# Attention: exponentials and combination a step later, in front of the next scores, on four one-bank PSUM tiles

## The chip, the cores and the metric

The kernel runs on one core of a Trainium2 chip. The metric is device time in microseconds (us) of one execution; lower is better. The engines are PE (TensorE matmul, with PEld its weight loads), DVE (VectorE), ACT (ScalarE), POOL (GpSimd) and SP (SyncE, which here issues DMAs).

## The reference

Two layers of a diffusion transformer over 512 image tokens and 256 context tokens of width 1024. Layer 0 mixes tokens by differential attention, layer 1 by a gated scan (HGRN2); each layer has a SwiGLU FFN before and behind the mixer. The change concerns layer 0's attention, with 8 heads, each of two maps of key width 64 and values of width 128:

```python
def attend(q, k, v):
    s = jnp.einsum('bqhmd,bkhmd->bhmqk', q, k).astype(jnp.float32) * scale
    p = jax.nn.softmax(s, axis=-1)
    a = (p[:, :, 0] - lam * p[:, :, 1]).astype(v.dtype)
    return jnp.einsum('bhqk,bkhe->bqhe', a, v)

def finish(o):
    o = rmsnorm(o, subln) * (1 - lam_init)
    return o.reshape(bsz, o.shape[1], DA_WIDTH) @ w_o

k_all = jnp.concatenate([k_l, k_c], axis=1)      # image tokens, then context
y_l = finish(sweep_query_blocks(lambda qb: attend(qb, k_all, v_all), q_l))
y_c = finish(attend(q_c, k_c, v_c)) if need_ctx else None
```

Queries are taken in blocks of 128. The four image blocks see all 768 keys ("wide" below), the two context blocks only the 256 context keys ("narrow"). Before attention q, k and v are projected, and q and k of the image tokens are rotated (RoPE).

## The kernel before

Matmuls are of fp32 precision put together from halves: every operand is split into a high part (an fp32r cast, on ScalarE, `split`) and a low part (the difference, on VectorE, `low`), and each product is three passes, high by high, high by low, low by high. Weights come by DMA in the order of a list of jobs (`J`); a job's splitting is done when it is asked for (`J.need`) or by `work()` ahead of need, as far as `J.limit` lets it.

Attention goes by pairs of heads, p = 0 to 3. The main line of the program is the projection of q, k and v of pair p (lines L593 and L1190), each 512 columns into a one-bank PSUM tile `tp`. Rotations of q and k (`rot`, L1137 to L1141) are VectorE's, the copy of the context part (`cx`, L1147) ScalarE's. Under it runs the attention of the pair before, as a generator `attn(p, vh)`, which a `Ticker` T moves on by one step for each T.every us of main-line matmuls (by the program's own count). `T.later(x, f)` calls f when x us more have been counted. The last pair's attention runs in this way under the output stage, `o_groups`, whose matmuls (L681) multiply the finished heads `on` (in `hT` and `hl` parts) by the output weight `wo`; in its part for y the products stand in `tp` tiles, which ScalarE or VectorE adds up in `y` (L694, L698).

`attn` has 12 items, two heads hh by six query blocks t, and takes three steps for each; a period is one item. In the kernel before:

- Step 1: the scores of item idx, two maps, each in a two-bank PSUM tile `mm` (L989, L995); the row maxima `nm` on VectorE (L999); the exponentials `pt` on ScalarE (L1004), which read the scores from PSUM and need the maxima. Then the value product of an earlier block if one is due (`av`, L1048, with its copy `of`, L1053), and the low parts that were put off (`settle`).
- Step 2: the transposes of item idx - 1 (L1031), six of 128x128 in two `tp` tiles, their high casts `aT` on ScalarE (L1033) and low parts on VectorE (L1037). These read `tp` from PSUM, so a tile is free when its low part is done.
- Step 3: the combination of item idx: reciprocal `rc` (L1013), factor `c1` (L1015), and pt[0] += c1 * pt[1] (L1016), all on VectorE; then a value weight's splitting, and `work()`.

So transposes already stand a period behind their scores. `finish` (L1061 to L1079) is the norm of a head: squares, their sums by TensorE, a power on GpSimd, and a broadcast product.

PSUM has eight banks of 2 KB a partition. All through the program they are two `mm` tiles of two banks, three `tp` tiles of one, and one tile `gv` of one bank, of which the value product uses one half and the norm the other. A tile is handed out again when its last reader is done. Each engine works in program order; the order is set by the generator's steps and by where T stands on the main line.

## Time and profile before

| what | value |
|---|---|
| time, median of 3 runs | 3121.38 us (3120.86 to 3123.49) |
| profiled execution | 3116.74 us |
| its span, first to last instruction | 3114.9 us |
| mean granted TensorE clock | 0.989 |
| PE busy | 3003.0 us, 96% of the span |
| PEld busy | 2703.4 us, 87% |
| DVE busy | 1718.1 us, 55% |
| ACT busy | 951.6 us, 31% |
| attention with scores in it | about 664 to 1060 us of the span |

The profile is of one execution. "Busy" is the time in which an engine works on something; the rest is idle, and a row says in brackets how long an engine idled before it and which instruction (engine, tile, line) ended the idle time. L12 is line 12 of the kernel; a name such as `tp<-hT,hl` says which tile is written from which. The granted clock is a share of TensorE's full speed; the levels seen here are 0.50 and 1.00, other values are means over a stretch that holds both.

### The profile page before, as it was taken

Reading aid. Unit: us, or ns where it says so; the run is one execution under the profiler, and the core shown is the slowest. Engines: PE = TensorE matmul, PEld = TensorE weight load, DVE = VectorE, ACT = ScalarE, POOL = GpSimd, SP = SyncE. Lnnn points to the kernel's source line nnn. Section 1 sums busy time; section 2 is a strip of 40 time slices with the busy share of each in tenths; the row PEclk is TensorE's granted clock in tenths of the full one; section 3 lists DMA queues with packets and bytes.
Section 4 is the critical chain, followed back from the end, with each engine's and each line's share of the span. In section 5 each row is a group of like instructions: output and inputs, shape, how many; then the busy total and the mean of one; then the engine's idle time right before and its main releaser. Section 6 shows DMA issues by size and latency. Waiting matters only on the chain.

```text
span 3114.9 us, 41080 instructions
## 1 busy us (share of the span) xinstructions
PE 3003.0 (96%) x17122; PEld 2703.4 (87%) x17122; DVE 1718.1 (55%) x2433; ACT 951.6 (31%) x1575; POOL 115.3 (4%) x187
## 2 busy tenths in 40 slices
PE   7999999999988999999999999999999999899998
PEld 5999999887876789999998999999889998678887
DVE  4555555656665774444448554444566475744344
ACT  4111111534444441111115111111544343442222
POOL 0000000100000100000001000000100000100000
PEclk9999999999999999999999999999999999999999
DMA  5333333245434323233222333333211110423231
GB/s 226 109 117 114 122 114 119 105 134 131 121 81 120 134 99 103 97 102 102 88 82 80 114 122 111 110 116 114 88 58 52 57 55 31 149 95 102 82 115 61
DMA packets 109546, 321.77 MB, mean 103 GB/s; under 512 B 11728, under 2 KB 12208, under 8 KB 109360
## 3 DMA queue, kind: packets, MB, share of 16 engines
q1 hardware_dynamic: 104432, 301.26, 30.1%
q0 software_dynamic: 3200, 11.59, 1.0%
q10 hardware_dynamic: 1728, 6.29, 0.5%
q8 instruction: 135, 2.21, 0.3%
q14 instruction: 51, 0.42, 0.0%
HBM read 292.83 MB, written 26.26 MB: 102 GB/s over the span
## 4 chain that ended last, share of the span: by engine, by line
PE 85%; DVE 5%; ACT 5%; issue 3%; DMA 1%; POOL 1%; SPq 0%; ACTq 0%; DVEq 0%; POOLq 0%
PE mm L602 34%; PE mm L681 21%; PE mm L593 9%; PE tp L593 5%; PE tp L602 3%; PE tp L1190 2%; PE tp L1423 2%; PE gv L1048 1%; PE tp L681 1%; PE mm L1333 1%; ACT pt L1004 1%; ACT tmp L564 1%; ACT tmp L414 1%; DVE nm L999 1%; PE mm L989 1%
## 5 line engine op out<-in xcount | busy, mean ns | idle before, releaser
L602 PE MATMUL mm<-hT,hl 128*128 128x384 f32 x6048 | 1067.3, 337 | 0.8 <-ACT tmp L773 0.8
L602 PEld LDWEIGHTS mm<-hT,hl 128*128 128x128 f32 x6048 | 1049.4, 188 | 9.7 <-issue 6.0
L681 PE MATMUL mm<-wo,a 128*128 128x512 f32 x2886 | 664.9, 390 | 0.5 <-DVE wo L194 0.5
L681 PEld LDWEIGHTS mm<-wo,a 128*128 128x128 f32 x2886 | 539.7, 188 | 115.6 <-DVE y L696 2.8
L698 DVE TENSOR_TENSOR y<-y,mm 128x1024 f32<-128x1024 f32 x163 | 199.1, 1221 | 496.8 <-PE mm L681 496.7
L194 DVE TENSOR_TENSOR hl<-raw,hl 128x1024 fp32r<-128x1024 f32 x250 | 302.5, 1221 | 138.2 <-ACT hl L203 137.8
L593 PE MATMUL mm<-hT,hl 128*128 128x512 f32 (+1 forms) x1680 | 335.2, 355 | 7.3 <-DVE hT L569 3.2
L593 PEld LDWEIGHTS mm<-hT,hl 128*128 128x128 f32 x1680 | 274.9, 190 | 60.1 <-DVE hT L569 6.8
L311 DVE SCALAR_TENSOR_TENSOR acc<-mw,cs,acc 128x512 f32<-128x512 f32 x392 | 271.7, 747 | 2.3 <-DMA mw<-in_w_mod_dram 0.7
L203 ACT CAST a<-tmp 128x768 fp32r<-128x768 f32 (+1 forms) x88 | 68.8, 781 | 660.1 <-DVE tmp L790 660.1
L203 ACT CAST hl<-raw 128x1024 fp32r<-128x1024 f32 x250 | 258.5, 1046 | 24.3 <-DMA raw<-in_w_in_dram 19.6
L593 PE MATMUL tp<-hT,hl 128*128 128x512 f32 (+1 forms) x1056 | 237.0, 371 | 15.5 <-DVE aT L1037 9.5
L203 ACT CAST wo<-raw 128x1024 fp32r<-128x1024 f32 x94 | 98.2, 1045 | 463.1 <-PE mm L681 457.7
L593 PEld LDWEIGHTS tp<-hT,hl 128*128 128x128 f32 x1056 | 173.5, 192 | 47.8 <-DVE aT L1037 11.4
L773 ACT ACTIVATE tmp<-mm 128x768 f32<-128x768 f32 (+1 forms) x88 | 66.8, 759 | 402.8 <-PE mm L602 339.8
L790 DVE TENSOR_TENSOR tmp<-tmp,mm 128x768 f32<-128x768 f32 (+1 forms) x88 | 78.0, 886 | 197.3 <-PE mm L602 141.6
L602 PE MATMUL tp<-hT,hl 128*128 128x384 f32 x768 | 147.1, 342 | 6.7 <-ACT F L1438 6.7
L602 PEld LDWEIGHTS tp<-hT,hl 128*128 128x128 f32 x768 | 131.3, 188 | 8.7 <-ACT F L1438 8.6
L1004 ACT ACTIVATE pt<-mm,nm 128x768 f32<-128x768 f32 (+1 forms) x96 | 72.4, 757 | 160.5 <-DVE nm L999 160.5
L194 DVE TENSOR_TENSOR a<-tmp,a 128x768 fp32r<-128x768 f32 (+1 forms) x88 | 78.5, 892 | 74.6 <-ACT a L203 74.6
L194 DVE TENSOR_TENSOR wo<-raw,wo 128x1024 fp32r<-128x1024 f32 x94 | 114.9, 1222 | 3.6 <-ACT wo L203 3.6
L681 PE MATMUL tp<-hl,hT 128*128 128x512 f32 x300 | 89.7, 432 | 13.6 <-DVE hl L194 6.3
(193 smaller groups left out, 2521.8 us busy)
## 6 DMA issues: line engine op xcount, KB each, us to landing
raw<-in_w_in_dram SPq DMA_DIRECT2D x176, 512.0 KB, 4.3
mw<-in_w_mod_dram SPq DMA_DIRECT2D x144, 512.0 KB, 4.3
raw<-in_w_out_dram SPq DMA_DIRECT2D x88, 512.0 KB, 3.2
raw<-in_hg_w_dram SPq DMA_DIRECT2D x32, 512.0 KB, 3.2
raw<-in_da_qk_dram SPq DMA_DIRECT2D x16, 512.0 KB, 3.5
gg<-gg_d POOLq DMA_DIRECT2D x12, 512.0 KB, 4.4
xp<-x_d SPq DMA_DIRECT2D x10, 512.0 KB, 8.1
raw<-in_da_v_dram SPq DMA_DIRECT2D x8, 512.0 KB, 3.3
```

The lines of the kernel that those rows point to most:

```text
L194: nc.vector.tensor_tensor(out=dst_lo, in0=src, in1=dst_hi.bitcast(F32), op=ALU.subtract)
L203: nc.scalar.copy(out=dst_hi, in_=src)
L311: nc.vector.scalar_tensor_tensor(out=acc[:, m], in0=raw[:, kk], scalar=cs[:, k, m:m + 1], in1=acc[:, m], op0=ALU.mult, op1=ALU.add)
L593: nc.tensor.matmul(out=ps_ap, lhsT=w[a], rhs=mv[b], start=(k == 0 and i == 0), stop=(k == nk - 1 and i == 2))
L602: nc.tensor.matmul(out=ps, lhsT=w[:, u, k], rhs=hT[:, k, v, a:b], start=(k == 0 and i == 0), stop=(k == KC - 1 and i == 2))
L681: nc.tensor.matmul(out=po if small else po[:, hh * 512:(hh + 1) * 512], lhsT=aT[ci][:, u, t * P:(t + 1) * P], rhs=wos[ci][:, v, hh * 512:( ...
L698: nc.vector.tensor_tensor(out=dst, in0=dst, in1=src, op=ALU.add)
L773: nc.scalar.activation(out=flat(sg, pgv), in_=pgv, func=AF.Silu)
L790: nc.vector.tensor_tensor(out=flat(sg, puv), in0=flat(sg, puv), in1=puv, op=ALU.mult)
L1004: nc.scalar.activation(out=pt[:, :n], in_=scs[m][:, :n], func=AF.Exp, bias=nms[m], accum_out=s0s[hh][:, t:t + 1] if m == 0 else s1)
L1190: nc.tensor.matmul(out=pv[:, tt], lhsT=hT[:, k, a, t * P:(t + 1) * P], rhs=wk[:, b], start=(k == 0 and i_ == 0), stop=(k == KC - 1 and i_ ...
L1423: nc.tensor.matmul(out=pv[:, tt], lhsT=hT[:, k, a, t * P:(t + 1) * P], rhs=wk[:, b], start=(k == 0 and i_ == 0), stop=(k == KC - 1 and i_ ...
```

## The change

Step 1 of the generator keeps scores and maxima, followed by `settle()` and then the value product. The exponentials move to the end of step 2, behind the transposes and casts of the item before, and the combination moves from step 3 to directly behind them. PSUM is dealt by stage: in attention there are two `mm` and four `tp` tiles and no `gv`; the value product and the norm take `tp` tiles. Before and behind that stage the deal is as it was. Beside this: the sums of the rotation are put off (0.3), its high and low parts go from 1.2 and 2.4 to 1.6 and 2.8; `wo(h)` is listed ahead of `on(h)`, for both mixers; J.limit is one higher in the last pair's projections; the output stage ticks every 35/56 instead of 34/56 us, and one step of the generator is called ahead of the first output matmul.

```diff
@@ -85,18 +85,27 @@
     def tmp(shape, dtype=F32):
         return cur["tmp"].tile(shape, dtype, tag="tmp", name="tmp")
 
-    mmp = ctx.enter_context(pool("ps_mm", 2, PSUM))
-    tpp = ctx.enter_context(pool("ps_tp", 3, PSUM))
-    gvp = ctx.enter_context(pool("ps_gv", 1, PSUM))
+    banks = {}
+
+    def deal(key, **bufs):
+
+        if "stack" in banks:
+            banks.pop("stack").close()
+        st = banks["stack"] = ExitStack()
+        for tag, n in bufs.items():
+            banks[tag] = st.enter_context(pool(f"ps_{tag}{key}", n, PSUM))
+
+    ctx.callback(lambda: banks.pop("stack").close())
+    deal(0, mm=2, tp=3, gv=1)
 
     def ps_mm(shape):
-        return mmp.tile(shape, F32, tag="mm", name="mm")
+        return banks["mm"].tile(shape, F32, tag="mm", name="mm")
 
     def ps_tp(shape):
-        return tpp.tile(shape, F32, tag="tp", name="tp")
+        return banks["tp"].tile(shape, F32, tag="tp", name="tp")
 
     def ps_gv(shape):
-        return gvp.tile(shape, F32, tag="gv", name="gv")
+        return banks["gv"].tile(shape, F32, tag="gv", name="gv")
 
     x_d = dram.tile([NT, P, D], F32, name="x_d")
     gg_d = [dram.tile([2, D], F32, name=f"gg_d{i}") for i in range(6)]
@@ -644,8 +653,8 @@
             J.add((tag + "wo", h), wsrc[h * P:(h + 1) * P, :], [P, D], conv_unit if h < TAIL else conv_wo, unit=h < TAIL)
 
         for h in range(TAIL):
+            wo(h)
             on(h)
-            wo(h)
         limits[tag + "o"] = len(J.jobs)
         for h in range(TAIL, HEADS):
             wo(h)
@@ -975,7 +984,7 @@
 
             s0s = {}
 
-            def scores_softmax(hh, t):
+            def scores(hh, t):
                 n = NTOK if t < LT else NCTX
                 st_ = stk[p, hh]
                 if t == 0:
@@ -998,6 +1007,10 @@
                     nm = sm.tile([P, 1], F32, tag="nm", name="nm")
                     nc.vector.tensor_reduce(out=nm, in_=scs[m][:, :n], axis=AX.X, op=ALU.max, negate=True)
                     nms.append(nm)
+                state[hh, t] = (scs, nms, s1, n)
+
+            def exps(hh, t):
+                scs, nms, s1, n = state[hh, t]
                 pts = []
                 for m in range(2):
                     pt = dp.tile([P, NTOK], F32, tag=f"p{m}", name="pt", bufs=2 - m)
@@ -1041,7 +1054,7 @@
             def av(hh, b):
 
                 aT = aTs.pop((hh, b))
-                ot = gv[:, 0]
+                ot = ps_tp([P, 256])
                 ks = list(range(NT)) if b < 2 else [LT, LT + 1]
                 for n_, kk in enumerate(ks):
                     for i_, (u, v) in enumerate(PASSES):
@@ -1062,13 +1075,14 @@
                 sq = dp.tile([P, NTOK], F32, tag="sq", name="sq", bufs=1)
                 nc.scalar.activation(out=sq, in_=of, func=AF.Square)
                 yield
-                ot = gv[:, 1]
+                ot = ps_tp([P, NT])
                 for j in range(NT):
                     nc.tensor.matmul(out=ot[:, j:j + 1], lhsT=sq[:, j * P:(j + 1) * P], rhs=ones, start=True, stop=True)
                 nc.vector.scalar_tensor_tensor(out=r, in0=ot[:, 0:NT], scalar=1.0 / P, in1=e, op0=ALU.mult, op1=ALU.add)
                 nc.gpsimd.tensor_tensor(out=r, in0=r, in1=halfc.to_broadcast([P, NT]), op=ALU.pow)
                 yield
                 for j0 in range(0, NT, 2):
+                    ot = ps_tp([P, 256])
                     for j in range(2):
                         nc.tensor.matmul(out=ot[:, j * P:(j + 1) * P], lhsT=r[:, j0 + j:j0 + j + 1].to_broadcast([P, P]),
                                          rhs=ident, start=True, stop=True)
@@ -1080,15 +1094,16 @@
 
             n = len(items)
 
+
             for idx in range(n + 2):
                 if idx < n:
-                    scores_softmax(*items[idx])
+                    scores(*items[idx])
+                settle()
                 if avs:
                     h2, b2 = avs.pop()
                     av(h2, b2)
                     if b2 == 2:
                         fin.append(finish(h2))
-                settle()
                 if idx == 0:
                     stack_q(p, 1)
                     stack_k(p, 1)
@@ -1098,9 +1113,10 @@
                     transp(h1, t1)
                     if t1 % 2 == 1:
                         avs.append((h1, t1 // 2))
+                if idx < n:
+                    exps(*items[idx])
+                    combine(*items[idx])
                 yield
-                if idx < n:
-                    combine(*items[idx])
                 if splits:
                     defer[0] = True
                     splits.pop(0)()
@@ -1121,11 +1137,11 @@
         avs = []
         fin = []
         splits = []
-        gv = ps_gv([P, 2, 256])
-
         T = Ticker()
         for p in range(NPAIR):
             T.every = 45.5 / 42
+            if p == NPAIR - 1:
+                J.limit += 1
             for wi, w in enumerate("qk"):
                 qs = 0.125 if w == "q" else 1.0
                 rot = {}
@@ -1136,15 +1152,16 @@
                     for j in range(2):
                         nc.vector.scalar_tensor_tensor(out=dst[:, j], in0=src, scalar=qs, in1=CSt[:, j ^ ab],
                                                        op0=ALU.mult, op1=ALU.mult)
-                    if ab:
-                        for j in range(2):
-                            nc.vector.tensor_tensor(out=rot[0][:, j], in0=rot[0][:, j], in1=dst[:, j],
-                                                    op=ALU.add if j else ALU.subtract)
 
                 def plain(ab, src, rot=rot, qs=qs):
                     if ab == 0:
                         rot["cx"] = pp.tile([P, 2, NCTX], F32, tag="cx", name="cx")
                     nc.scalar.activation(out=rot["cx"][:, ab], in_=src, func=AF.Copy, scale=qs)
+
+                def sums(rot=rot):
+                    for j in range(2):
+                        nc.vector.tensor_tensor(out=rot[0][:, j], in0=rot[0][:, j], in1=rot[1][:, j],
+                                                op=ALU.add if j else ALU.subtract)
 
                 def highs(rot=rot):
                     hl = rot["hl"] = pp.tile([P, 2, 2, NTOK], F32R, tag="qkhl", name="qkhl")
@@ -1168,6 +1185,8 @@
                         plain(ab, first[ab][:, NLAT:NTOK])
                         rotate(ab, first[ab][:, 0:NLAT])
                         continue
+                    if p == 0 and ab == 0:
+                        deal(1, mm=2, tp=4)
                     u = need_spread(("dqk", p, wi, ab), 2)
                     for (a0, a1) in ((0, NLAT), (NLAT, NTOK)):
                         pl = ps_tp([P, 512])
@@ -1176,8 +1195,9 @@
                             rotate(ab, pl)
                         else:
                             plain(ab, pl[:, 0:NCTX])
-                T.later(1.2, highs)
-                T.later(2.4, stored)
+                T.later(0.3, sums)
+                T.later(1.6, highs)
+                T.later(2.8, stored)
             vh = [dp.tile([P, NT, 2, P], F32R, tag="vh", name="vh", bufs=3) for _ in range(2)]
             wv = [J.need(("dv", p, 0)), need_spread(("dv", p, 1), 1)]
             for t2_ in range(NT // 2):
@@ -1209,11 +1229,13 @@
         cur["yo"] = y
         cur["oT"] = new_hT()
         J.limit = limits["do"]
-        T.every = 34.0 / 56
+        T.every = 35.0 / 56
+        T(T.every)
         outs = o_groups("d", [(0,), (1, 2), (3, 4)], "yo", NT, T)
         while T.gen is not None and next(outs, outs) is not outs:
             pass
         T.finish()
+        deal(2, mm=2, tp=3, gv=1)
 
     def mixer_tail(l, tag, si, nt, nxt, fp, xp, outs):
```

In TensorE's order nothing moves in the first three pairs, apart from the name of the tile of value products and norms. The three places below show the instructions as they stand in each engine's queue, with repeated ones counted.

First, ScalarE in the middle of pair 1, about 783 to 795 us of the trace before. L1004 (before) and L1017 (after) are exponentials, L1033 and L1046 casts of transposes, L1053 and L1066 copies of a value product, L203 and L212 casts of weights, L1147 and L1159 copies of a projection. Before:

```order
L1004 ACTIVATE pt,s_6176<-mm,nm 128x768
L1004 ACTIVATE pt,s_6373<-mm,nm 128x768
L1053 COPY of<-gv 128x256
L1033 CAST aT<-tp 128x3x128 x2
L203 CAST hl<-raw 128x1024
L1004 ACTIVATE pt,s_6176<-mm,nm 128x256
L1004 ACTIVATE pt,s_6460<-mm,nm 128x256
L1033 CAST aT<-tp 128x3x128 x2
L1147 ACTIVATE cx<-tp 128x256
```

After:

```order
L1066 COPY of<-tp 128x256
L1046 CAST aT<-tp 128x3x128 x2
L1017 ACTIVATE pt,s_6194<-mm,nm 128x768
L1017 ACTIVATE pt,s_6394<-mm,nm 128x768
L212 CAST hl<-raw 128x1024
L1046 CAST aT<-tp 128x3x128 x2
L1017 ACTIVATE pt,s_6194<-mm,nm 128x256
L1017 ACTIVATE pt,s_6481<-mm,nm 128x256
L1159 ACTIVATE cx<-tp 128x256
```

In each period the two exponentials have gone from ahead of the copy and the casts of the transposes to behind them.

Second, ScalarE where the output stage begins, at 955 us of the trace before; L694 and L703 empty output tiles into y, and the casts of `hT` and `hl` (L203, L212) split the finished heads and the output weight. Before:

```order
L1195 CAST vh<-tp 128x2x128 x2
L203 CAST hT<-raw 128x768
L203 CAST hl<-raw 128x1024
L1004 ACTIVATE pt,s_8158<-mm,nm 128x768
L1004 ACTIVATE pt,s_8159<-mm,nm 128x768
L694 COPY y<-tp 128x512 x2
L203 CAST hT<-raw 128x768
L203 CAST hl<-raw 128x1024
L1004 ACTIVATE pt,s_8158<-mm,nm 128x768
L1004 ACTIVATE pt,s_8221<-mm,nm 128x768
L694 COPY y<-tp 128x512
L1033 CAST aT<-tp 128x3x128 x2
```

After:

```order
L1215 CAST vh<-tp 128x2x128 x2
L1017 ACTIVATE pt,s_8198<-mm,nm 128x768
L1017 ACTIVATE pt,s_8199<-mm,nm 128x768
L212 CAST hT<-raw 128x768
L703 COPY y<-tp 128x512 x2
L212 CAST hl<-raw 128x1024
L212 CAST hT<-raw 128x768
L1046 CAST aT<-tp 128x3x128 x2
L1017 ACTIVATE pt,s_8198<-mm,nm 128x768
L1017 ACTIVATE pt,s_8255<-mm,nm 128x768
L703 COPY y<-tp 128x512 x3
```

The first exponentials now stand ahead of the cast of the first finished head, and the first output weight is no longer split here.

Third, TensorE at the same place: L1190 and L1210 are the last value projection, L681 and L690 output matmuls, L989 to L1004 scores. Before:

```order
L1190 MATMUL tp<-hl,hT 128x256 x27
L681 MATMUL tp<-hl,hT 128x512
L989 MATMUL mm<-stk 128x512
L989 MATMUL mm<-stk 128x256
L989 MATMUL mm<-stk 128x512
L989 MATMUL mm<-stk 128x256
L995 MATMUL mm<-stk 128x512 x2
L995 MATMUL mm<-stk 128x256 x2
L681 MATMUL tp<-hl,hT 128x512 x3
```

After:

```order
L1210 MATMUL tp<-hl,hT 128x256 x27
L998 MATMUL mm<-stk 128x512
L998 MATMUL mm<-stk 128x256
L998 MATMUL mm<-stk 128x512
L998 MATMUL mm<-stk 128x256
L1004 MATMUL mm<-stk 128x512 x2
L1004 MATMUL mm<-stk 128x256 x2
L690 MATMUL tp<-hl,hT 128x512 x2
```

The last pair's first scores have gone ahead of the first output matmul.

## Rows read from the trace of the kernel before

**Rows 1.** Windows of the two parts: us, busy by engine (instructions), PEclk, DMA share, GB/s

```profile
...
664.00:955.00 291.00, 266.07 (x1779) 231.21 (x1777) 186.46 (x347) 125.92 (x287) 9.72 (x10) 0.98 0.41 109
955.00:1060.00 105.00, 85.78 (x453) 67.25 (x453) 70.14 (x128) 48.38 (x102) 6.90 (x8) 0.92 0.28 81
...
```

**Rows 2.** TensorE's waits, 664 to 1060: us in total, times, longest us

```profile
...
PE tp L593 <- DVE aT L1037: 9.5, 6, 2.4
PE tp L1031 <- ACT y L694: 7.8, 3, 4.8
PE tp L593 <- ACT cx L1147: 4.1, 3, 1.8
PE tp L1031 <- ACT cx L1147: 3.6, 3, 1.7
PE tp L681 <- DVE aT L1037: 2.6, 4, 0.8
PE gv L1048 <- DVE r L1068: 2.4, 1, 2.4
PE tp L681 <- ACT hl L203: 2.4, 1, 2.4
PE tp L1031 <- DVE y L698: 2.0, 2, 1.8
PE mm L989 <- ACT pt L1004: 1.6, 2, 1.3
...
```

**Rows 3.** Windows at clock 0.50: first of four and sum, last of three and sum

```profile
...
686.12:689.53 3.41, 3.21 (x15) 3.21 (x16) 3.34 (x9) 0.00 (x0) 0.00 (x0) 0.50 0.48 159
...
sum 13.64, PE 13.32 PEld 12.42 DVE 9.80 ACT 3.08 POOL 1.33; mean PE 3.33 PEld 3.10 DVE 2.45 ACT 0.77 POOL 0.33
...
1013.80:1017.21 3.41, 3.41 (x12) 2.39 (x10) 2.94 (x7) 1.49 (x3) 0.00 (x0) 0.50 0.00 0
sum 17.06, PE 13.21 PEld 10.45 DVE 12.40 ACT 7.29 POOL 0.00; mean PE 4.40 PEld 3.48 DVE 4.13 ACT 2.43 POOL 0.00
```

**Rows 4.** Timeline, 780 to 800: start us, us, operation, [idle before it <- releaser]

```profile
...
782.72 1.82 DVE L999 TENSOR_REDUCE nm<-mm 128x1 f32<-128x768 f32 x2 [0.95 <-PE mm L995]
783.72 0.90 ACT L1004 ACTIVATE pt<-mm,nm 128x768 f32<-128x768 f32 x1 [4.31 <-DVE nm L999]
...
785.53 0.36 ACT L1053 COPY of<-gv 128x256 f32<-128x256 f32 x1
...
786.26 0.82 PE L1031 MATMUL tp<-ident,pt 128*128 128x128 f32 x6
786.78 0.86 ACT L1033 CAST aT<-tp 128x384 fp32r<-128x384 f32 x2 [0.89 <-PE tp L1031]
...
787.30 1.02 DVE L1037 TENSOR_TENSOR aT<-tp,aT 128x384 fp32r<-128x384 f32 x2 [2.75 <-ACT aT L1033]
...
788.68 1.02 DVE L1016 SCALAR_TENSOR_TENSOR pt<-pt,c 128x768 f32<-128x768 f32 x1
...
789.47 0.39 PE L989 MATMUL mm<-stk 128*128 128x256 f32 x2
...
794.97 2.63 PE L593 MATMUL tp<-hT,hl 128*128 128x512 f32 x6 [1.82 <-ACT cx L1147]
...
```

**Rows 5.** Groups by line on ScalarE, 664 to 1060: busy us, mean ns, idle before

```profile
...
L1004 ACT ACTIVATE pt<-mm,nm 128x768 f32<-128x768 f32 (+1 forms) x96 | 72.4, 757 | 160.5 <-DVE nm L999 160.5
...
```

**Rows 6.** Timeline of the output stage's start, 955 to 957

```profile
...
955.11 0.85 ACT L203 CAST hT<-raw 128x768 fp32r<-128x768 f32 x1
...
955.84 1.06 ACT L203 CAST hl<-raw 128x1024 fp32r<-128x1024 f32 x1
...
956.95 0.50 PE L681 MATMUL tp<-hl,hT 128*128 128x512 f32 x1 [2.41 <-ACT hl L203]
...
```

**Rows 7.** Timeline of TensorE in the output stage, at 1004 and 1013

```profile
...
1004.42 1.41 PE L681 MATMUL tp<-hl,hT 128*128 128x512 f32 x5
...
1013.09 0.55 PE L1031 MATMUL tp<-ident,pt 128*128 128x128 f32 x3 [1.78 <-DVE y L698]
...
```

## The prediction, made before the changed kernel had run

> **What bounds the kernel now.** I read the windows first, then the waits of TensorE inside them, then the granted clock, then one period in the timeline. Attention's scores run from about 664 to 1060 us. In its two parts TensorE is busy 266.07 of 291.00 us and 85.78 of 105.00 us [rows 1]: idle 24.9 and 19.2, together 44.1 us. VectorE is busy 186.46 and 70.14 us there and ScalarE less, so neither is the limit on the average; TensorE is, and what can be won is its idle time and its slow time. The waits say who ended the idle time [rows 2]: there are 17 rows of 43.9 us in all, the nine shown have 36.0 us. Six of the nine (9.5, 7.8, 4.1, 3.6, 2.6 and 2.0, together 29.6) are one thing: TensorE wants a one-bank PSUM tile ("tp") that ScalarE or VectorE has not yet emptied. Seven stretches stand at a granted clock of 0.50, that is 1.2 instead of 2.4 GHz; TensorE is busy 13.32 us in the four under the projections and 13.21 in the three of the output stage, 26.53 us in all, work that takes half of it at 2.4 GHz, so 13.3 us are lost [rows 3]. The last begins at 1013.80, 0.7 us after a wait of 1.78 us ended [rows 3, 7], the first at 686.12, beside one of the waits of 2.4; I take all of them for a consequence of the idle time. Ceiling of the stage: 44.1 + 13.3 = 57.4 us.
>
> Why the banks come late is to be seen in one period [rows 4]. The exponentials stand at 783.72 in ScalarE's queue as soon as the scores are written; they wait for the maxima (VectorE, 782.72, 1.82 us). Behind them stand the copy of the value product (785.53) and the casts of the transposes (786.78). In the next period the projection's own emptying (cx) stands behind them too, and TensorE idles 1.82 us for it (794.97). Summed up, ScalarE idles 160.5 us in front of exponentials [rows 5], and all that is queued behind them waits as well.
>
> **The change part by part.** *Exponentials behind the casts.* Row for row TensorE's order in the three pairs under the projections stays, so its work stays. ScalarE now empties the value product and the transposes first and does the exponentials after, when the maxima are long there; the emptying of projection (cx) and of output tiles (y) no longer stands behind a waiting instruction. Of the 29.6 us I leave 4: in the first period of the output stage two weight casts now stand ahead of the casts of the transposes, 1.06 + 0.85 us on ScalarE [rows 6], and their two low parts ahead on VectorE, for which I count 2.2 us of wait at the norm product; some 1.8 remain elsewhere. **Gain 25.6.**
>
> *What is late instead.* The scores' two tiles are freed only by the exponentials, which now start when the casts of the transposes end. From rows 4: last transpose ends 787.08, casts end 787.64, and two exponentials take 1.81 (783.72 to 785.53), so the second tile is free at 789.45 and, with 0.1 us for the release (it shows as 0.05 in rows 6: the cast ends at 956.90, the matmul starts at 956.95), at 789.55. The next scores begin at 789.47 and reach the second tile 0.2 to 0.4 later: hidden, with nothing to spare. Where fewer matmuls lie between, it shows: five output matmuls take 1.41 us [rows 7], against 2.4 needed. Counted by period: three of 0.25, one of 0.2, two of 0.85 and one of 0.4 in the output stage (3.1), some 0.3 in each of six periods under the projections (1.9). Together 5.0, in place of the 1.6 that the scores wait now. **Cost 3.4.** Bounds: zero, and at most 1.81 in each of the 32 wide periods, 58.
>
> *The combination directly behind them* (reciprocal, factor, 1.02 us of multiply-add) makes VectorE wait for the exponentials. Queued behind it are the rotations, the norm product and the next maxima. Per wide period: the low parts of the transposes end at 788.32, the exponentials at 789.45: 1.1 us of waiting, 32 times, and some 0.4 in 16 narrow ones, 42 us. VectorE's busy time is 256.6 of 396 us [rows 1], so it fits; the combination ends 789.45 + 1.4 = 790.9, as the next scores end, and the next transposes stand another 1.5 us behind that. I value this at zero. Bounds: if that cover goes, 42 us; gain: none, since no transposes wait for it now.
>
> *Four one-bank tiles, value product and norm in them too.* The product waited 2.4 us for the norm's reader because both lay in one tile [rows 2]; that goes. Cost of the added takers: I find the ones before each taker emptied at least a step earlier, so nothing. **Gain 2.4**, bounds 0 and 2.4.
>
> *Start of the output stage.* Now the first output matmul waits 2.41 us for casts that begin at 955.11 [rows 6]. After, the first scores come ahead of it, and on ScalarE the first exponentials ahead of the cast of the output's input. So after the scores TensorE waits for the first maximum (0.1 + 0.9), two exponentials (1.81), the cast (0.85) and the release: 3.8, and 0.4 more for its low part behind the combination. 4.2 instead of 2.4: **cost 1.8.** That the first weight is split beforehand hides nothing of it. In pair 0 a value weight's low part comes behind the combination: **cost 0.6.** Bounds for both: 0 and 6.
>
> *Sums, high and low parts of the rotation a little later, weight before input, a tick of 35 instead of 34:* VectorE and ScalarE work of the same length, used several us later; nothing.
>
> *The other waits* (7.9 us, the eight rows after the nine of the list) I leave as they are.
>
> *The clock.* If the stretches follow idle time, the four in the pairs go (half of 13.32 us, since hardly a wait is left there by the steps above), and of the three in the output stage one or two stay behind the 4.2 us: some 4 of 13.3 us remain. **Gain 9.3**, bounds 0 and 13.3.
>
> Sum: 25.6 − 3.4 + 2.4 − 1.8 − 0.6 + 9.3 = 31.5 us. The profiled execution took 3116.7 us; its sum is 3085.2. The median of the three timed runs lies 4.6 us above that execution, so the median to expect is 3089.9, say **3089 us**.
>
> **Rivals.** *The waits change their name (part of the gain).* The chain of scores, maxima, casts, exponentials, scores becomes the period. For it: the 0.0 to 0.1 us to spare in rows 4, and a collision or two per pair with a weight cast of 1.06 us [rows 6]. Against it: ScalarE is busy only 174 of 396 us. If the chain costs 0.5 us in each of the 32 wide periods (16 instead of 5) and half the clock loss stays (6.6 instead of 4), the gain is 31.5 − 11 − 2.6 = 17.9: 3103 us.
>
> *Everything goes.* All waits for tiles, the start, and the clock: 57.4 less the 7.9 of other waits: 49.5, 3072 us. For it: the order leaves slack in most places; against it the start of the output stage.
>
> *VectorE becomes the limit (the other side).* Place: the combination's wait in every wide period. If the maxima of the next scores come behind it so late that exponentials wait again, the exponentials lie bare between transposes and scores: 1.81 x 32 = 58 us, less the 29.6 + 2.4 that go in any case and with the clock as now: 26 us slower, 3147; the point from which it decides is about 1.1 us per wide period (32 x 1.1 = 35, what is won without the clock plus part of it). Against it: from rows 4 the first maximum could start at 790.9 + 0.9 = 791.8, and the exponentials behind it are not due before the casts of the next transposes (790.9 + 1.5 + 0.82 + 0.56 = 793.8): about 2 us of room, in which one queued operation of VectorE fits.
>
> *Nothing happens*, because TensorE's order in the pairs is the same and the waits are bound by VectorE's low parts (9.5 us of them) rather than by ScalarE: 3121. Against it: those low parts themselves idle for the casts behind the exponentials.
>
> *The room is larger than idle time.* On the rows, idle and slow time is all there is, since no matmul goes and none gets shorter. Weight loads are busy 231.21 + 67.25 = 298.5 of 396 us [rows 1], which would leave 97.5 us: 3117 − 97.5 + 4.6 = 3024. The Trainium skill (Perfetto Trace Analysis, "Identifying the Most-Contended Engine") says that TensorE's room is to be judged by the busy share of weight loads, not by that of matmuls. No run here shows that this room can be had; the change touches no matmul, and I give it 1 in 100.
>
> **How the numbers follow.** Forecast 3089 with a chance of 0.58; part of the gain, 3103, 0.22; everything, 3072, 0.12; VectorE as the limit 0.04; nothing 0.03; the larger room 0.01. The forecast's own range is 3081 to 3097. Between 3073 and 3107 lie the forecast, the part and most of the way to the full gain, some 8 in 10. About 0.2% (6 us) is what a measurement of this kernel can tell from no change: faster by more 0.91, within it 0.04, slower 0.05 (VectorE, and a bit of what I don't see).
>
> **What would show it.** Right: the waits of TensorE for "tp" tiles behind casts, cx and y fall from 29.6 us to some 4; the idle time of ScalarE before exponentials falls from 160.5 us to below 50; a new wait of the reciprocal for exponentials of some 40 us on VectorE; scores waiting for exponentials about 5 us; a wait of about 4 us at the first output matmul; the granted clock of 664 to 955 at 1.00. Wrong: scores waiting for exponentials 15 us and more, transposes waiting for the combination, a clock at 0.50 in the pairs without idle time ahead of it, or idle time that has moved behind 1060 us.

## The result

The changed kernel takes 3083.06 us (median of 4 runs, 3081.9 to 3085.34), the kernel before 3121.12 us (4 runs, 3118.22 to 3123.49): a ratio of 0.9886, 95% interval 0.9872 to 0.9899. (The two medians alone give 0.9878; in the later rounds the kernel before stands at 3117.97 to 3119.15 us, so the gain is rather 35 than 38 us.) The forecast was 3089 us, in a range of 3073 to 3107. The time came out within 6 us of the forecast; the largest of the reasons given for it held only in part.

The profiled execution took 3081.90 us, 34.8 less than that of before, with a span of 3080.1 us. Measured between the same matmuls of both traces, 0.5 us were won ahead of attention, some 25 in the three pairs under the projections, some 9 in the output stage, 0.3 behind it. The windows of the two parts, at the same places of the program as in [rows 1] (whose boundary of 955 is 954.5 by this count):

```profile
663.50:928.90 265.40, 259.65 (x1780) 227.21 (x1779) 186.65 (x348) 125.11 (x286) 10.11 (x10) 0.99 0.47 124
928.90:1025.50 96.60, 84.25 (x452) 64.00 (x452) 68.46 (x127) 47.42 (x102) 6.90 (x8) 0.96 0.25 78
```

The work is the same; TensorE's idle time went from 44.1 us in the two parts together to 5.8 and 12.4 us. Its waits, as in [rows 2]:

```profile
PE tp L1087 <- DVE aT L1050: 4.8, 5, 2.7
PE tp L690 <- ACT hT L212: 3.8, 1, 3.8
PE tp L1210 <- DVE aT L1050: 2.1, 2, 1.4
PE tp L1080 <- DVE y L707: 1.2, 1, 1.2
...
PE mm L998 <- ACT pt L1017: 0.8, 3, 0.3
```

All rows together make 17.8 us instead of 43.9. Waits for the projection's copies (cx) and for output tiles that ScalarE empties are gone, and so are waits of the q and k projections (L602) for low parts of transposes. New are the norm's broadcasts (L1087) that wait for low parts of transposes. Two stretches at a clock of 0.50 are left of seven [rows 3]:

```profile
674.40:677.82 3.42, 3.42 (x12) 2.26 (x11) 0.24 (x1) 0.00 (x0) 0.00 (x0) 0.50 0.45 153
933.82:940.64 6.82, 6.74 (x23) 5.72 (x25) 1.84 (x3) 0.61 (x2) 1.34 (x1) 0.50 0.26 85
sum 10.24, PE 10.16 PEld 7.98 DVE 2.08 ACT 0.61 POOL 1.34; mean PE 5.08 PEld 3.99 DVE 1.04 ACT 0.31 POOL 0.67
```

So 5.1 instead of 13.3 us are lost to the clock in this execution. The changed kernel was profiled a second time (run e5 below); there the waits make 17.1 us, but four stretches stand at 0.50:

```profile
sum 20.48, PE 19.62 PEld 14.35 DVE 7.33 ACT 3.70 POOL 2.69; mean PE 4.91 PEld 3.59 DVE 1.83 ACT 0.93 POOL 0.67
```

That is 9.8 us lost, and that execution took 3087.86 us: what the clock takes differs between executions of one kernel. Back to the first trace: the exponentials' idle time on ScalarE, against [rows 5], by line:

```profile
L1017 ACT ACTIVATE pt<-mm,nm 128x768 f32<-128x768 f32 (+1 forms) x96 | 72.6, 769 | 14.2 <-DVE nm L1008 14.2
```

And the period that answers to [rows 4], in the timeline of pair 1:

```profile
772.07 1.81 DVE L1008 TENSOR_REDUCE nm<-mm 128x1 f32<-128x768 f32 x2
...
774.09 0.37 ACT L1066 COPY of<-tp 128x256 f32<-128x256 f32 x1 [3.83 <-PE tp L1061]
775.28 0.82 PE L1044 MATMUL tp<-ident,pt 128*128 128x128 f32 x6
775.81 0.86 ACT L1046 CAST aT<-tp 128x384 fp32r<-128x384 f32 x2 [1.35 <-PE tp L1044]
...
776.55 0.92 ACT L1017 ACTIVATE pt<-mm,nm 128x768 f32<-128x768 f32 x1
...
777.44 0.92 ACT L1017 ACTIVATE pt<-mm,nm 128x768 f32<-128x768 f32 x1
...
778.48 0.16 DVE L1026 RECIPROCAL rc<-s 128x1 f32<-128x1 f32 x1 [1.14 <-ACT pt L1017]
778.49 0.40 PE L998 MATMUL mm<-stk 128*128 128x256 f32 x2
```

The copy of the value product and the casts come as soon as TensorE has written. The maxima end at 773.88, the exponentials begin 2.7 us later and wait for nothing; the second ends at 778.36, 0.1 us before the next scores begin, and the reciprocal waits 1.14 us for it.

### The profile page after: what moved, and what is told of

Its sections match the earlier page's. It is cut to its first block, busy times and chain, and to the rows that moved or that the text cites. A ratio compares the mean times of both kernels' runs of the same rounds, so it can differ in the third digit from the quotient of the medians.

```text
span 3080.1 us, 41105 instructions
## 1 busy us (share of the span) xinstructions
PE 2994.0 (97%) x17122; PEld 2694.4 (87%) x17122; DVE 1715.6 (56%) x2433; ACT 950.1 (31%) x1575; POOL 115.4 (4%) x187
## 4 chain that ended last, share of the span: by engine, by line
PE 86%; DVE 4%; ACT 4%; issue 3%; DMA 2%; POOL 1%; SPq 1%; ACTq 0%; DVEq 0%; POOLq 0%
PE mm L611 34%; PE mm L690 21%; PE mm L602 9%; PE tp L602 6%; PE tp L611 3%; PE tp L1445 2%; PE tp L1210 1%; PE tp L1061 1%; PE tp L690 1%; PE mm L1355 1%; ACT tmp L423 1%; ACT tmp L573 1%; PE mm L998 1%; DMA mw<-in_w_mod_dram 1%; PE mm L1004 1%
## 5 line engine op out<-in xcount | busy, mean ns | idle before, releaser
L690 PE MATMUL mm<-wo,a 128*128 128x512 f32 x2886 | 665.0, 390 | 0.5 <-DVE wo L203 0.5
L690 PEld LDWEIGHTS mm<-wo,a 128*128 128x128 f32 x2886 | 539.6, 188 | 115.7 <-DVE y L705 2.7
L203 DVE TENSOR_TENSOR hl<-raw,hl 128x1024 fp32r<-128x1024 f32 x250 | 302.3, 1220 | 141.4 <-ACT hl L212 141.2
L602 PE MATMUL mm<-hT,hl 128*128 128x512 f32 (+1 forms) x1680 | 334.2, 354 | 7.0 <-DVE hT L578 3.1
L602 PEld LDWEIGHTS mm<-hT,hl 128*128 128x128 f32 x1680 | 273.8, 189 | 59.8 <-DVE hT L578 6.9
L212 ACT CAST a<-tmp 128x768 fp32r<-128x768 f32 (+1 forms) x88 | 68.7, 781 | 659.9 <-DVE tmp L799 659.9
L212 ACT CAST hl<-raw 128x1024 fp32r<-128x1024 f32 x250 | 258.4, 1047 | 24.5 <-DMA raw<-in_w_in_dram 18.9
L212 ACT CAST wo<-raw 128x1024 fp32r<-128x1024 f32 x94 | 98.3, 1045 | 463.0 <-PE mm L690 457.7
L602 PE MATMUL tp<-hT,hl 128*128 128x512 f32 (+1 forms) x1056 | 232.4, 366 | 1.9 <-DVE hl L203 1.0
L602 PEld LDWEIGHTS tp<-hT,hl 128*128 128x128 f32 x1056 | 170.5, 188 | 31.9 <-issue 3.7
L203 DVE TENSOR_TENSOR a<-tmp,a 128x768 fp32r<-128x768 f32 (+1 forms) x88 | 78.5, 892 | 74.6 <-ACT a L212 74.6
L203 DVE TENSOR_TENSOR wo<-raw,wo 128x1024 fp32r<-128x1024 f32 x94 | 114.9, 1222 | 3.6 <-ACT wo L212 3.6
L690 PE MATMUL tp<-hl,hT 128*128 128x512 f32 x300 | 88.9, 426 | 9.6 <-ACT hT L212 4.0
L1008 DVE TENSOR_REDUCE nm<-mm 128x1 f32<-128x768 f32 (+1 forms) x96 | 70.1, 771 | 23.9 <-PE mm L1004 23.9
```

The costliest lines, as they stand in the source:

```text
L203: nc.vector.tensor_tensor(out=dst_lo, in0=src, in1=dst_hi.bitcast(F32), op=ALU.subtract)
L212: nc.scalar.copy(out=dst_hi, in_=src)
L602: nc.tensor.matmul(out=ps_ap, lhsT=w[a], rhs=mv[b], start=(k == 0 and i == 0), stop=(k == nk - 1 and i == 2))
L690: nc.tensor.matmul(out=po if small else po[:, hh * 512:(hh + 1) * 512], lhsT=aT[ci][:, u, t * P:(t + 1) * P], rhs=wos[ci][:, v, hh * 512:( ...
L1008: nc.vector.tensor_reduce(out=nm, in_=scs[m][:, :n], axis=AX.X, op=ALU.max, negate=True)
```

## The experiments

Each kernel was timed in five rounds beside the kernel before on its chip (4 to 11 runs each). What is compared is the ratio to that kernel; the changed kernel itself has 0.9886 and, in e5, 0.9892.

| run | what differs from the changed kernel | median us | ratio, 95% interval |
|---|---|---|---|
| e1_old_order | order of before | 3102.66 | 0.9948 (0.9934 to 0.9962) |
| e2_old_banks | PSUM deal of before | 3109.22 | 0.9968 (0.9957 to 0.9980) |
| e3_combine_third | combination in step 3 | 3081.37 | 0.9881 (0.9867 to 0.9894) |
| e4_late_exponentials | ScalarE copies ahead of exponentials | 3115.41 | 0.9992 (0.9983 to 1.0001) |
| e5_changed_again | nothing | 3084.39 | 0.9892 (0.9879 to 0.9906) |
| e6_rest_alone | order and deal of before | 3120.61 | 1.0007 (0.9998 to 1.0016) |
| e7_old_start | start of the output stage of before | 3084.85 | 0.9891 (0.9875 to 0.9906) |
| e8_input_first | first head split before first scores | 3081.04 | 0.9882 (0.9868 to 0.9895) |
| e9_old_rotation | times of the rotation's parts of before | 3085.69 | 0.9891 (0.9877 to 0.9906) |
| e10_old_jobs | jobs of before | 3084.70 | 0.9890 (0.9875 to 0.9905) |
| e11_input_first_norm_early | e8, norm's steps in step 1 | 3081.68 | 0.9880 (0.9865 to 0.9894) |
| e12_input_first_combine_third | e8 and e3 together | 3076.65 | 0.9866 (0.9850 to 0.9883) |

**e1: the old order, with four tiles.**

```diff
                     scores(*items[idx])
-                settle()
+                    exps(*items[idx])
...
+                settle()
...
+                yield
                 if idx < n:
-                    exps(*items[idx])
                     combine(*items[idx])
-                yield
```

> The changed kernel with ScalarE's and VectorE's old order alone: exponentials directly behind the maxima in step 1, combination in step 3, put-off low parts behind the value product. Four one-bank tiles and all else as changed. Theory A (the order on ScalarE is the cause): most of the gain goes, the exponentials idle more than 120 us for the maxima again, TensorE's waits for tp tiles come back to some 20 to 30 us, clock stretches at 0.50 come back in the pairs; 3108 to 3118 us. Rival B (the fourth one-bank tile is the cause, and takes up late casts): 3083 to 3092 us, waits for tp below 12 us.

TensorE's waits here:

```profile
PE tp L1044 <- ACT of L1066: 4.9, 4, 2.2
PE tp L690 <- ACT hT L212: 3.8, 1, 3.8
PE tp L1087 <- DVE aT L1050: 3.1, 5, 1.1
PE tp L690 <- ACT y L703: 2.5, 2, 1.4
PE tp L1087 <- ACT y L703: 2.5, 1, 2.5
```

Neither theory holds: 0.9948 lies between them, so the order is worth 17 to 19 us where the four tiles are in place. The exponentials idle 150.1 us for the maxima again, and ScalarE's emptying is late. But what VectorE ends, 19.5 us of the waits of before and 9.5 in the first row of [rows 2] alone, is 5.9 us here.

**e2: the old deal, with the new order.**

```diff
-                ot = ps_tp([P, 256])
+                ot = gv[:, 0]
...
-                ot = ps_tp([P, NT])
+                ot = gv[:, 1]
...
-                    if p == 0 and ab == 0:
-                        deal(1, mm=2, tp=4)
...
```

> The changed kernel with the old deal of PSUM alone: three one-bank tp tiles, and value product and norm in the two halves of one gv tile. Theory A: the product waits for the norm's reader again (2.4 and 0.9 us), projections have one tile less, while the 4.8 us that the norm's broadcasts wait for low parts in the changed trace go; 3081 to 3091 us. Rival B (the fourth tile is the cause): tp waits above 20 us, 3100 us or more.

```profile
PE tp L602 <- DVE aT L1050: 7.6, 5, 2.0
PE tp L690 <- DVE aT L1050: 5.3, 4, 2.5
PE gv L1061 <- DVE of L1089: 4.5, 5, 2.8
...
PE tp L1208 <- DVE aT L1050: 2.5, 4, 0.8
```

Again neither theory gives the time, and it lies nearer to the rival: 0.9968, so some 25 us of the gain need the new deal. The waits are VectorE's now: 15.4 us for low parts and 4.7 for the shared tile gv. One of them in the timeline of this run:

```profile
861.03 1.82 DVE L1008 TENSOR_REDUCE nm<-mm 128x1 f32<-128x768 f32 x2 [1.83 <-PE mm L1004]
861.73 0.81 PE L1044 MATMUL tp<-ident,pt 128*128 128x128 f32 x6
862.25 0.86 ACT L1046 CAST aT<-tp 128x384 fp32r<-128x384 f32 x2 [3.70 <-PE tp L1044]
862.77 1.22 DVE L203 TENSOR_TENSOR hl<-raw,hl 128x1024 fp32r<-128x1024 f32 x1
...
863.90 1.01 DVE L1050 TENSOR_TENSOR aT<-tp,aT 128x384 fp32r<-128x384 f32 x2
864.50 1.83 PE L602 MATMUL tp<-hT,hl 128*128 128x256 f32 x10 [1.96 <-DVE aT L1050]
```

The casts end at 863.1, early. The low parts, which free the two tiles of the transposes, stand on VectorE behind the maxima and a weight's low part until 863.90, and the projection wants its next tile 1.4 us before that. Here ScalarE is not what is late; with four tiles the projection has another one to take. The fourth tile and the parting of value product and norm were not timed apart.

The kernel before has nearly the same wait, with the old order, in its timeline at 866 to 870:

```profile
867.58 1.21 DVE L194 TENSOR_TENSOR hl<-raw,hl 128x1024 fp32r<-128x1024 f32 x1
868.64 0.85 ACT L1033 CAST aT<-tp 128x384 fp32r<-128x384 f32 x2
869.15 1.02 DVE L1037 TENSOR_TENSOR aT<-tp,aT 128x384 fp32r<-128x384 f32 x2 [0.36 <-ACT aT L1033]
869.76 1.12 PE L593 MATMUL tp<-hT,hl 128*128 128x256 f32 x6 [2.41 <-DVE aT L1037]
```

The casts stand behind the exponentials here, but VectorE is busy with a weight's low part until 0.36 us before it can take the transposes' own: of the 2.41 us that TensorE waits, earlier casts could have saved no more than that. In the four longest waits of the first row of [rows 2] (2.41, 2.41, 1.70 and 1.66 us) the low parts idle 0.35, 0.36, 0.36 and 1.44 us for the cast.

**e3: the combination in step 3**, exponentials where the change puts them.

```diff
                     exps(*items[idx])
+                yield
+                if idx < n:
                     combine(*items[idx])
-                yield
```

> The changed kernel with the combination in step 3 again, exponentials where the change puts them. The prediction valued the combination's place at zero. Theory A: 3080 to 3087 us; VectorE's wait of the reciprocal for exponentials falls from 26.5 us to under 10, TensorE's waits change by under 3 us in sum. Rival C (the combination's wait holds up the queue behind it): 2 to 8 us faster than the changed kernel. Rival D (the place counts the other way, transposes wait for the combination): 3090 us or more, with waits of transposes for pt.

0.9881 beside 0.9886 and 0.9892: the combination's place is worth nothing that can be measured, as theory A has it. Its number for VectorE missed: the reciprocal's wait fell only from 26.5 to 18.6 us, not below 10. Two transposes waited for the combination, 1.2 us in all.

**e4: exponentials made late** at six places.

```diff
                     pt = dp.tile([P, NTOK], F32, tag=f"p{m}", name="pt", bufs=2 - m)
+                    if m == 0 and p < NPAIR - 1 and (hh, t) in ((0, 2), (1, 1)):
+                        for _ in range(4):
+                            nc.scalar.copy(out=pt[:, :n], in_=scs[m][:, :n])
```

> The changed kernel with four copies of the scores (some 0.9 us each on ScalarE, overwritten by the exponentials behind them) ahead of the exponentials in two periods of each of the first three pairs, six places. In the changed trace the exponentials end 0.8 to -0.3 us before the next scores there. Theory A (nothing to spare, and slow clock follows idle time): next scores wait about 3.4 us at each place, 20 us in all, and stretches at 0.50 appear behind some of the six, 1.7 us each; 3103 to 3114 us. Rival E (slack is larger than it looks): under 10 us of new waits, below 3094 us. Rival F (the clock does not follow idle time): the waits come, but no stretch at 0.50 begins within 4 us behind them; 3100 to 3104 us.

The first place in TensorE's timeline, and three of the clock's windows:

```profile
688.95 0.61 PE L998 MATMUL mm<-stk 128*128 128x512 f32 x2 [2.37 <-ACT pt L1020]
689.83 1.01 PE L998 MATMUL mm<-stk 128*128 128x512 f32 x2 [0.27 <-ACT pt L1020]
```

```profile
689.72:696.55 6.83, 6.72 (x28) 5.85 (x29) 5.53 (x9) 0.43 (x2) 0.00 (x0) 0.50 0.01 2
727.26:730.67 3.41, 3.41 (x13) 2.54 (x14) 3.34 (x7) 2.44 (x4) 0.00 (x0) 0.50 0.01 2
...
819.42:826.25 6.83, 6.83 (x21) 4.78 (x22) 3.42 (x7) 1.88 (x4) 0.00 (x0) 0.50 0.18 39
```

The six waits are 2.37, 2.38, 2.31, 2.75, 1.59 and 2.74 us, 14.1 together: less than the 20 expected. The four copies took 3.32 us and not 3.6, and at the first place 2.37 + 0.27 us of that show, so 0.7 us were spare: the scores begin when the first of their two tiles is free, one exponential earlier than I had counted. At five of the six, all but that of 1.59, a stretch at 0.50 begins between 0.2 us ahead and 2.2 us behind the wait's end; TensorE is busy 27.03 us in these, 13.5 lost. So rivals E and F fall, and of theory A the mechanism holds, not the sizes: in these five the idle TensorE cost about as much again in clock. Five more stretches stand in this trace where nothing was copied, one at 846.73 and four in the output stage; TensorE is busy 23.1 us in them, against 10.2 in all of the changed kernel's. The time, 3115.41 us, lies 1 us above A's range.

**e5 and e6: the changed kernel again, and the rest alone.** e6 is the edits of e1 and e2 together.

> The changed kernel once more, on the chip of the three kernels below, as their measure: ratio to the kernel before 0.986 to 0.990.

> The changed kernel with both the old order on ScalarE and VectorE and the old deal of PSUM; what stays changed is the start of the output stage, the later sums and parts of the rotation, the order of the jobs and the tick of 35/56. From the runs before, order + rest gave some 9 us, tiles + rest some 16, all together some 36. Theory A2 (the rest is worth nothing, and order and fourth tile each need the other: a tile is late when either ScalarE's cast or VectorE's low part is late): within 4 us of the kernel before, tp waits ended by VectorE's low parts 10 to 16 us and by ScalarE's y and cx 12 to 18. Rival H (the parts simply add: order 20, tiles 27, so the rest costs 11): 8 to 14 us slower than before.

e5 repeats the changed kernel's time (0.9892). In e6 the rest is worth nothing (1.0007), so rival H falls. That each part needs the other, as theory A2 says, does not follow either: against e6 the order alone gives 0.0039 (12 us), the tiles alone 0.0059 (18 us), together 30 of some 36; what is left is within what the intervals leave open. The waits in attention say the same, by who ended them (us, over all rows of each run; "others" are casts and low parts of weights and heads, and GpSimd):

| kernel | by ScalarE's emptying | by VectorE's reading | others | PE busy at 0.50 |
|---|---|---|---|---|
| before | 18.6 | 19.5 | 5.8 | 26.5 |
| rest alone (e6) | 12.5 | 24.9 | 6.9 | 43.4 |
| order + rest (e2) | 2.9 | 25.7 | 7.2 | 23.7 |
| tiles + rest (e1) | 14.3 | 5.9 | 6.8 | 38.5 |
| all (changed) | 0.8 | 9.8 | 7.2 | 10.2 |

The order takes ScalarE's waits and leaves VectorE's; the tiles take VectorE's and leave ScalarE's. The columns show one execution each and do not give the times exactly: for the order alone, waits and half of the busy time at 0.50 fall by 18 us, where its timing gives 12.

**e7: the old start of the output stage.**

```diff
-        T.every = 35.0 / 56
-        T(T.every)
+        T.every = 34.0 / 56
```

> The changed kernel with the old start of the output stage: a tick of 34/56 us and no step of the generator ahead of the first output matmul. Theory (the prediction's term: the new start costs 1.8): the wait before the first output matmul is 2.4 instead of 3.8 us, 0 to 3 us faster than the changed kernel on the same chip. Rival: first scores behind the first matmul let later periods run closer together, 1 to 5 us slower.

The same time (0.9891 and 0.9892), so neither the theory's gain nor the rival's loss can be seen. The first wait fell to 1.5 us, but a wait of 2.4 us for low parts and one of 1.9 of scores for exponentials stand behind it:

```profile
PE mm L998 <- ACT pt L1017: 2.5, 3, 1.9
PE tp L690 <- DVE aT L1050: 2.4, 1, 2.4
...
PE tp L690 <- ACT hT L212: 1.5, 1, 1.5
```

**e8: the first head split ahead of the first scores.**

```diff
+        J.upto(J.pos["don", 0] + 1)
         T(T.every)
```

> The changed kernel, but the first finished head is split (cast of hT on ScalarE, low part on VectorE) ahead of the generator's step that stands before the first output matmul. TensorE's order stays. The wait of 3.8 us before that matmul goes to under 1, and the stretch at 0.50 that begins there (6.8 us, TensorE busy 6.74, so 3.4 lost) may go: 3 to 7 us faster than the changed kernel on the same chip. Rival: the first maxima and exponentials come about 1 us later and a wait behind them takes the place: within 1.5 us of it.

The wait went to 0.2 us, and the median is 3.4 us lower than e5's, but the intervals overlap: theory and rival stay undecided. Three stretches at 0.50 stand in the output stage all the same (13.7 us busy), the first at 932.43 with no wait above 0.3 us in the 9 us of TensorE's timeline ahead of it.

**e9 and e10: rotation and jobs as before.**

```diff
+                    if ab:
+                        for j in range(2):
...
-                T.later(0.3, sums)
-                T.later(1.6, highs)
-                T.later(2.8, stored)
+                T.later(1.2, highs)
+                T.later(2.4, stored)
```

```diff
+            on(h)
             wo(h)
-            on(h)
...
-            if p == NPAIR - 1:
-                J.limit += 1
```

> The changed kernel with the rotation's sums, high and low parts at their old times (sums with the rotation, 1.2, 2.4). The prediction valued the delays at zero. Theory: ratio to before 0.986 to 0.991, as the changed kernel (0.9886 and 0.9892). Rival: the two sums of 0.68 us again stand ahead of low parts of transposes on VectorE, and waits of tp tiles for VectorE grow by 4 us or more: 0.991 or above.

> The changed kernel with the finished head listed ahead of its output weight again and the jobs' limit not raised, so that the first output weight is split at the start of the output stage. The prediction valued this part at zero. Theory: the weight's cast (1.06 us on ScalarE) and low part come behind the cast of the head, the first wait grows by about 1 us, to 4.8: ratio 0.988 to 0.991. Rival: nothing beyond the noise, 0.987 to 0.989, first wait 3.8 still.

0.9891 and 0.9890: neither can be told from the changed kernel, and in e9 the waits of tiles for VectorE did not grow. In e10 the first wait is 4.7 us as expected, with 1.1 for the low part behind it.

**e11 and e12: two attempts to go on from e8.** e12 is the edits of e8 and e3; e11 is that of e8 and the following, where `work()`, in attention, does not split a job but moves a head's norm on by one step:

```diff
                         fin.append(finish(h2))
+                work()
...
                     defer[0] = False
-                work()
                 yield
```

> The kernel of the run with the first head's split ahead of the first scores, and the norm's steps moved from step 3 to step 1, behind the value product, so that its broadcasts no longer ask for a tile right behind the transposes. There these waited 4.3 us for low parts. Theory (the wait belongs to the place, two tiles being held by the transposes): it falls below 1 us, transposes wait at most 2 us more for the norm's product instead; 1 to 5 us faster than the changed kernel, ratio 0.985 to 0.988. Rival: the wait moves to the transposes in full, ratio 0.988 to 0.990.

> The first head's split ahead of the first scores, and the combination in step 3. Theory: the two are independent, 3 us and 1 us off the changed kernel: ratio 0.986 to 0.988. Rival: the combination in step 3 takes back what the split gives, ratio 0.988 to 0.990.

In e11 the broadcasts no longer wait for low parts, but projections wait 2.2 us for the norm's product and scores 3.4 for exponentials: 0.9880, on the line between theory and rival. e12 has the lowest median, 3076.65 us, and its four runs (3076.1 to 3078.67) lie below all eight of the changed kernel, though on another chip than e5's; the intervals of the ratios still overlap, so that it is faster is not shown. No stretch at 0.50 lies in its pairs, and one in its output stage.

## Why the prediction was right, and where it was not

- **The ceiling and the sum.** 31.5 us forecast, 34.8 measured on the profiled executions; waits 26.1 and clock 8.2 make 34.3 of it. That no time is won outside idle and slow time held, so the rival of the larger room fell. The other half of the 6 us is the median: the forecast took over the 4.6 us by which the timed runs of the kernel before lay above its profiled execution, and for the changed kernel it is 1.2.
- **Exponentials behind the casts: the step that failed.** 25.6 us of tile waits were put down to the order, because the low parts seemed late only for the casts behind the exponentials. e1, e2 and e6 show otherwise: the order took ScalarE's part, the tiles VectorE's, and with its share of the clock the order is worth 12 us alone and 17 to 19 with the four tiles. In e2 the casts are early and the low parts are late for VectorE's own queue; at 869.15 in the kernel before, VectorE idled 0.36 us for the cast where TensorE waited 2.41. The prediction's example did not bear it out either: in [rows 4] the casts at 786.78 wait 0.89 us for TensorE's transposes and not behind the exponentials. The rival that nothing happens, the waits being bound by VectorE's low parts, was right on these waits, and the argument against it was this wrong step. Of the tile waits of 29.6 us, some 4 were to stay; 9.8 are left.
- **Four tiles.** Valued at 2.4 us with bounds 0 and 2.4; without them some 25 us of the gain are missing (e2), alone they give 18 (e1 against e6). That added takers cost nothing was wrong too: broadcasts and sums of the norm now wait 4.8 and 1.2 us, of which only the 2.7 of the point on the first period below were counted. Order and tiles came in one change and in one sum, so what one was given too much the other lacked; that the time was right all the same is luck. Of the order with the old tiles the prediction would have said some 3091 us, and e2 measured 3109.
- **Scores waiting for exponentials.** 5.0 us forecast, 0.8 measured. The prediction found nothing to spare; e4 shows 0.7 us at its first place. The rival that the waits change their name fell with it. Which of the periods counted for the 5.0 us went better than forecast was not followed up.
- **Combination.** A wait of 42 us on VectorE was forecast, at no cost; 26.5 us were measured, at no cost that e3 can tell. VectorE did not become the limit.
- **Start of the output stage.** 4.2 us forecast, 3.8 + 0.4 measured. As a cost of 1.8 it is right only for that wait: e7 gets the same time without it. The low part of a value weight in pair 0, valued at 0.6 us, cost 0.4.
- **First period of that stage.** 2.2 us were counted at the norm's product behind two casts and their low parts. The wait is there, 2.73 us, at the norm's broadcast.
- **Clock.** 9.3 us forecast; 8.2 measured in the first profiled execution and 3.5 in that of e5, so the agreement is partly that of a lucky execution. One stretch stayed in the pairs, where none was expected. The mechanism is supported by e4, and e8 shows that it is not the whole.

## What to carry to other kernels

Here, a reader of a PSUM tile that was late behind a waiting instruction was cured by another order, and one that was late in a full queue by another tile. The row of the wait names only the last reader and leaves open which it is; how long that reader itself had idled for its input, 0.36 of 2.41 us in the kernel before, tells. When several edits go together, the sum can be right while a term is ten times too small; undo each large edit alone, and both together. An order may put an instruction last that has time, such as exponentials whose result is needed a period later, if its release still comes before the next writer; in e4 what came later was paid nearly twice, once in waiting and once in clock.

## What was not expected of the hardware

Up to some 675 us the kernels hardly differ. The same two waits, 0.86 and 1.00 us near 673, are followed by a stretch at 0.50 in the changed kernel (674.40) and in e1, e3, e5, e6, e7 and e11, and by none in the kernel before and in e2, e4, e8, e9, e10 and e12. And a wait of 1.45 us for a low part before a value projection is followed by one in e4 (846.73, the wait ends at 844.91), by none in the changed kernel (824.05). The length of the idle time does not decide either, as two executions of the changed kernel show, the first profiled one and that of e5, at the same place:

```profile
945.74 0.68 PE L1087 MATMUL tp<-ident,r 128*128 128x128 f32 x4 [2.73 <-DVE aT L1050]
```

```profile
946.12 0.68 PE L1087 MATMUL tp<-ident,r 128*128 128x128 f32 x4 [1.94 <-DVE aT L1050]
946.75:950.16 3.41, 3.41 (x12) 2.15 (x10) 1.72 (x4) 0.95 (x2) 0.00 (x0) 0.50 0.51 188
```

No stretch follows the longer wait; one begins 0.6 us behind the end of the shorter. In e8 the clock fell without any wait above 0.3 us. Two microseconds ahead of that, TensorE had done the norm's twelve sums of one column each; it did the same in e12, behind the same wait of 0.22 us, and no stretch begins there. What decides it stays open.
